# Attention of a two-block network: where the softmax is divided by its sums

## Chip, cores and metric

The kernel runs on one core of a Trainium2 chip, as one launch. The metric is device microseconds of that core. Three timed runs of the kernel before gave 3551.97, 3553.97 and 3556.66 us; the median, 3553.97 us, is the time before.

## The reference, cut to what matters

Two blocks of layers follow each other, each with mixers and feed-forward parts, on 512 tokens of width 1024 (and 256 context tokens in the second). The change touches only the attention of the second block, which comes in three kinds: a windowed one with a sink (layer 0), a neighbourhood one with a table of biases, and a global one (both layer 1). For each head all three compute the same thing:

```
s = q @ k.T * scale (+ bias or mask)       # 128 queries by n keys
e = exp(s - max(s));  sums = e.sum(-1) (+ exp(sink - max))
o = (e / sums) @ v                          # 128 queries by 64
```

A number divided before the product with `v` or after it gives the same `o`.

## The kernel before

Two heads times 128 queries are one unit of attention. There are 56 units: 24 windowed ones (line 1321; 256, 512 or 640 keys) and 32 of layer 1 (line 1715; 768 keys each, 16 with the table of biases and 16 global). A unit has three stages, and `step` (line 975) interleaves the stages of three units that follow each other: while one unit computes scores, the one before is transposed and the one before that is multiplied with the values.

- Scores (line 927), for each of the two heads: TensorE multiplies queries and keys into a PSUM tile `sc`; VectorE takes the maximum (lines 1006 to 1011); ScalarE writes the exponentials into `scratchP` and their sums beside it (line 1012), and in the windowed units the exponential of the sink (line 1014).
- Transposes (line 948): VectorE adds the sink's part (line 944), takes the reciprocal of one column of sums (line 945) and the numerators of each head are multiplied by it (line 946): by VectorE for the first head of a unit, by GpSimd for the second. Then TensorE transposes 128x128 blocks (line 325) into a PSUM tile `pt`, four to a piece, and ScalarE, or VectorE for the second piece of a unit (`ptv`), copies each piece into `scratchPT` (line 958).
- Values (line 960): TensorE multiplies the transposed blocks with the values into a PSUM tile `o` (line 322), in which the output stands transposed: 64 rows for each head by 128 queries. ScalarE copies it to SBUF (line 968; `bos` in the windowed units, `ox` in the others), and SyncE's queue stores it.

PSUM has two `sc` tiles in the windowed part and three in layer 1, two and one `pt`, and a single `o` (lines 1825 and 1867). `new_scratch` (line 984) cuts two large SBUF tiles into 5 slots for numerators and 8 for transposed pieces.

The windowed units run beside the first steps of a recurrence (`recurrence`, line 1345): its products `PM` on TensorE, its copies `M` and `W` on ScalarE and a long run of small VectorE operations on a tile `X` (lines 1440 to 1444). The units of layer 1 run alone, but for weights that are loaded ahead. The order of the instructions on each engine is not that of the source: the framework sorts them when it builds the program, and each engine then takes its own in that order.

Of the kernel before, what the change touches and what calls it, by code (L numbers as in the profile page):

```python
# [10 lines left out]
F32 = mybir.dt.float32  # L11
# [4 lines left out]
ALU = mybir.AluOpType  # L16
AX = mybir.AxisListType
PSUM = bass.MemoryType.PSUM
MUL, ADD, SUB = ALU.mult, ALU.add, ALU.subtract

D = 1024
KD = 8
S = 512
# [11 lines left out]
CTX = 256  # L35
T2 = S + CTX
# [84 lines left out]
class Kernel:  # L121
# [794 lines left out]
    def attention(self, active, qs, keys, vals, out, store, masks=(), **k):  # L916

        nc = self.nc  # L920
        P = [None, None]
        nb = len(vals[0])
        blocks = [(p, b) for p in range(2) for b in range(nb)]
        pieces = [blocks[i:i + 4] for i in range(0, 2 * nb, 4)]
        PT = {}

        def scores(p):
            sc = self.ps.tile([128, S + CTX], F32, tag="sc", name="sc", bufs=self.nsc)
            first = S
            for i, (kh, kl) in enumerate(keys[p][::-1]):  # L930
                if i:
                    first -= kh.shape[1]
                s = sc[:, S:] if i == 0 else sc[:, first:S]
                mk = masks if i else ()
                self.mm(s, qs[:, p, :], kh, start=True, stop=False)
                self.mm(s, qs[:, p, :], kl, start=False, stop=not mk)
                for j, (c, m) in enumerate(mk):
                    nc.tensor.matmul(s[:, c:c + 128], self.identb, m, start=False, stop=j == len(mk) - 1)
            P[p] = self.softmax(sc[:, first:], **{x: y[p] for x, y in k.items()})

        def normalised(p):
            P[p], a, es = P[p]
            if es is not None:
                nc.vector.tensor_tensor(a, a, es, ADD)
            nc.vector.reciprocal(a, a)
            (nc.gpsimd if p else nc.vector).tensor_scalar(P[p], P[p], a, None, op0=MUL)

        def transposed(i):
            pt = self.ps.tile([128, 512], F32, tag="pt", name="pt", bufs=self.npt)
            t = self.scratch("PT")  # L950
            for p, b in pieces[i]:
                if b == 0:
                    normalised(p)
            for j, (p, b) in enumerate(pieces[i]):
                self.tr(pt[:, 128 * j:128 * j + 128], P[p][:, 128 * b:128 * b + 128])
                PT[p, b] = t[:, 128 * j:128 * j + 128]
            w = slice(0, 128 * len(pieces[i]))
            (nc.vector.tensor_copy if i in self.ptv else nc.scalar.copy)(t[:, w], pt[:, w])

        def weighted(j):  # L960
            if j == 0:
                PT["o"] = self.ps.tile([128, 128], F32, tag="o", name="o", bufs=self.no)
            o = PT["o"]
            for b in range(2 * j, min(2 * j + 2, nb)):
                for p in range(2):
                    self.mm(o[64 * p:64 * p + 64, :], vals[p][b], PT[p, b], start=b == 0, stop=b == nb - 1)
            if 2 * j + 2 >= nb:
                nc.scalar.copy(out, o)
                if store:
                    nc.sync.dma_start(*store)  # L970

        active.append([[partial(f, i) for i in range(n)] for f, n in ((scores, 2), (transposed, len(pieces)), (weighted, (nb + 1) // 2))])
        self.step(active)

# [6 lines left out]
                if i < len(t):  # L981
                    t[i]()

    def new_scratch(self, **n):

        self.ring = {}
        for (name, k), tag in zip(n.items(), ("hThi", "hTlo")):
            W = self.hp.tile([128, KD * S], F32, tag=tag, name=f"scratch{name}")
            w = KD * S // k
            self.ring[name] = [W[:, w * j:w * j + w] for j in range(k)]  # L990

    def scratch(self, name):
        r = self.ring[name]
        r.append(r.pop(0))
        return r[-1]

    def softmax(self, sc, bias=None, nsink=None, sink=None, scale=None):

        nc, v = self.nc, self.nc.vector
        st = self.small.tile([128, 8], F32, tag="sm", name="sm", bufs=8)  # L1000
        mx, nm, sums, es = (st[:, i:i + 1] for i in range(4))
        n = sc.shape[1]
        P = self.scratch("P")[:, :n]

        if bias is not None:
            v.tensor_tensor_reduce(sc[:, :S], sc[:, :S], bias, 1.0, -3e38, op0=ADD, op1=ALU.max, accum_out=mx)
            v.reduce_max(es, sc[:, S:], axis=AX.X)
            v.tensor_scalar(nm, mx, es, -1.0, op0=ALU.max, op1=MUL)
        else:
            v.reduce_max(mx, sc, axis=AX.X, negate=True)  # L1010
            v.tensor_scalar(nm, mx, scale if nsink is None else nsink, None, op0=MUL if nsink is None else ALU.min)
        nc.scalar.activation(P, sc, AF.Exp, bias=nm, accum_out=sums, scale=1.0 if scale is None else scale)
        if sink is not None:
            nc.scalar.activation(es, sink, AF.Exp, bias=nm)
        return P, sums, es if sink is not None else None


    def store_split(self, x, dst, key=False):
# [768 lines left out]
    def block2(self, n, xd, out, stop=None, dbg=None):  # L1787
        nc, ap = self.nc, self.ap
# [19 lines left out]
        for i in range(2):  # L1808
            nt = NT2 if i == 0 else NT
            esM = ExitStack()  # L1810
            if i == 0:
                es = ExitStack()
                gemm_pools(es, "in0")
                self.ntmp = 1
                self.load_consts(3, self.act)
                self.load_consts(6, self.act)
                hT = self.hT2(n, mods)
                st = self.even(hT)
                es.close()
                es = ExitStack()  # L1820
                R = self.act = self.pool("R", es)
                self.load_consts(4, R)
                esW = ExitStack()
                other_psum(esW, "w")
                self.nsc, self.npt, self.no, self.npp, self.ptv = 2, 2, 1, 1, (1,)
                self.new_scratch(P=5, PT=8)
                windowed = self.windowed(st, R)
                next(windowed)
                rest = self.recurrence(st, R)
                for _ in range(4):  # L1830
                    next(windowed)
                next(rest)
                list(windowed)
                esW.close()
                self.npp = 2
                other_psum(es, "r")
                next(rest, None)
                self.hT = self.hT_tile()
                acc = self.new_acc()
                self.dn = ("w", 4)  # L1840
                self.mix_out(i, st, acc, 1, NT2)
                self.dn = ("dn", 2)
                next(rest, None)
                es.close()
                if stop in ("rw", "b"):
                    nc.sync.dma_start(dbg.rearrange("(i p) t -> i p t", p=128), st["out"][0 if stop == "rw" else 1])
                    esM.close()
                    es2.close()
                    return
                es = ExitStack()  # L1850
                gemm_pools(es, "o0")
                self.ntmp, self.nxt = 2, 4
            else:
                M = self.pool("M", esM)
                es = ExitStack()
                gemm_pools(es, "in1")
                self.ntmp, self.nhid = 2, 1
                self.load_consts(3, M)
                hT = self.hT2(n, mods)
                st = self.odd(hT, M)  # L1860
                mods = self.mods2(i, 3, V[f"g_pre_ff{i}"])
                es.close()
                es = ExitStack()
                R = self.pool("R1", es)
                other_psum(es, "a")
                self.act = R
                self.nsc, self.npt, self.no, self.ptv = 3, 1, 1, (1,)
                self.new_scratch(P=5, PT=8)
                self.odd_attention(st)
                es.close()  # L1870
                if stop in ("c", "d"):
                    nc.sync.dma_start(dbg.rearrange("(i p) t -> i p t", p=128), st["out"][0 if stop == "c" else 1])
                    esM.close()
                    es2.close()
                    return
                es = ExitStack()
                gemm_pools(es, "o1")
                self.ntmp, self.nxt = 2, 4
                self.hT = self.hT_tile()
# [11 lines left out]
            es = ExitStack()  # L1891
# [7 lines left out]
            n = self.ffn2(i, hT, nt, done)  # L1899
# [38 lines left out]
```

## Time and profile before

| | us |
|---|---|
| median of three timed runs | 3553.97 |
| the profiled execution | 3566.74 |
| its span, first to last instruction | 3565.0 |
| windowed units, by the trace | 1646 to 1790 |
| units of layer 1, by the trace | 2957 to 3139 |
| TensorE busy over the span | 3316.1 (93%) |
| VectorE, ScalarE, GpSimd busy | 2062.1, 1308.6, 504.1 |

All durations are those of the profiled execution, which took 1.74 us more than its span and 12.77 us more than the median. Matmuls are pipelined, so the duration of one says less than the distance from one to the next. TensorE is one queue of matmuls (PE) with a queue of weight loads (PEld) that runs ahead of it. [...]

### The profile page before, as it was taken

To read this page: it belongs to the slowest core of one execution; us is meant where nothing else is said; L and a number is where in the kernel's file an instruction comes from. 1 tells how busy PE (TensorE), PEld (TensorE's weight loads), DVE (VectorE), ACT (ScalarE), POOL (GpSimd) and SP (SyncE) were. 2 spreads that over 40 slices of the span, in tenths; PEclk is the share of its full clock that TensorE was granted. 3 is DMA by queue.
4 is the path that set the end of the run, shared out by engine and by line. 5 is a ranking of instruction groups with operands and counts; after the bars stand their busy time and mean duration, and the time that the engine had idled before them with its cause. 6 is when DMAs were issued, how large, how long until landed. Compare 5 with 4: busy or idle time off the path is not lost. (4 is left out here: it accounts for less than half of the span.)

```text
span 3565.0 us, 50330 instructions
## 1 busy us (share of the span) xinstructions
PE 3316.1 (93%) x19975; PEld 2638.1 (74%) x19975; DVE 2062.1 (58%) x3796; ACT 1308.6 (37%) x2150; POOL 504.1 (14%) x274
## 2 busy tenths in 40 slices
PE   8989999878999998988888899999999989999998
PEld 5677767746776777866587897888888777778887
DVE  4674554897745557686767667433334726653334
ACT  3243333327333334443542245422222525653222
POOL 0020000540200000123343331010000103410001
PEclk9999999989999998997988799999999999999999
DMA  7645565440456333445222124661221474143332
GB/s 249 193 143 167 171 219 176 133 142 12 123 175 208 108 105 109 113 117 170 52 73 68 50 71 165 144 154 54 68 63 62 135 208 153 37 131 106 95 95 83
DMA packets 520693, 436.66 MB, mean 122 GB/s; under 512 B 91924, under 2 KB 450042, under 8 KB 518922
## 3 DMA queue, kind: packets, MB, share of 16 engines
q1 hardware_dynamic: 520458, 433.45, 40.3%
q8 instruction: 157, 2.57, 0.3%
q14 instruction: 78, 0.64, 0.1%
HBM read 368.96 MB, written 63.78 MB: 121 GB/s over the span
## 5 line engine op out<-in xcount | busy, mean ns | idle before, releaser
L301 PE MATMUL dnps<-whi_dn,hidh 128*128 128x512 f32 x1120 | 449.0, 401 | 2.4 <-ACT hidh L276 1.2
L302 PE MATMUL dnps<-wlo_dn,hidh 128*128 128x512 f32 x1120 | 445.9, 398 | 0.0
L303 PE MATMUL dnps<-whi_dn,hidl 128*128 128x512 f32 x1120 | 443.4, 398 | 1.0 <-DVE hidl L277 1.0
L289 DVE TENSOR_TENSOR wlo_dn<-wraw_dn,whi_dn 128x1024 fp32r<-128x1024 f32 x136 | 167.3, 1231 | 249.8 <-ACT whi_dn L288 249.7
L301 PE MATMUL upps<-hThi,whi_up 128*128 128x512 f32 (+1 forms) x768 | 297.8, 390 | 5.3 <-DVE hThi L276 5.3
L302 PE MATMUL upps<-hTlo,whi_up 128*128 128x512 f32 (+1 forms) x768 | 295.2, 385 | 5.3 <-DVE hTlo L277 5.3
L303 PE MATMUL upps<-hThi,wlo_up 128*128 128x512 f32 (+1 forms) x768 | 294.2, 384 | 0.0
L423 DVE TENSOR_TENSOR acc<-dnps,acc 128x512 f32<-128x512 f32 x200 | 136.9, 688 | 213.4 <-PE dnps L303 212.9
L301 PEld LDWEIGHTS dnps<-whi_dn,hidh 128*128 128x128 f32 x1120 | 211.0, 188 | 64.6 <-ACT hidh L276 5.6
L288 ACT CAST whi_dn<-wraw_dn 128x1024 fp32r<-128x1024 f32 x140 | 147.1, 1051 | 283.9 <-PE dnps L303 105.5
L302 PEld LDWEIGHTS dnps<-wlo_dn,hidh 128*128 128x128 f32 x1120 | 211.3, 189 | 53.2 <-issue 2.7
L303 PEld LDWEIGHTS dnps<-whi_dn,hidl 128*128 128x128 f32 x1120 | 210.7, 189 | 53.2 <-DVE hidl L277 3.3
L302 PE MATMUL up2ps<-hTlo,whi_ff 128*128 128x512 f32 (+1 forms) x576 | 215.8, 375 | 5.0 <-DVE hTlo L277 4.7
L301 PE MATMUL up2ps<-hThi,whi_ff 128*128 128x512 f32 (+1 forms) x576 | 213.9, 373 | 2.3 <-DVE hThi L276 2.3
L303 PE MATMUL up2ps<-hThi,wlo_ff 128*128 128x512 f32 (+1 forms) x576 | 215.4, 375 | 0.0
L289 DVE TENSOR_TENSOR wlo_up<-wraw_up,whi_up 128x1024 fp32r<-128x1024 f32 x88 | 110.6, 1257 | 141.0 <-ACT whi_up L288 141.0
L301 PEld LDWEIGHTS upps<-hThi,whi_up 128*128 128x128 f32 x768 | 147.0, 192 | 54.5 <-issue 11.9
L302 PEld LDWEIGHTS upps<-hTlo,whi_up 128*128 128x128 f32 x768 | 147.5, 192 | 42.7 <-issue 9.9
L823 POOL TENSOR_TENSOR ag<-acc,gg 128x1024 f32<-128x1024 f32 x20 | 48.7, 2437 | 904.5 <-DVE acc L423 873.3
L303 PEld LDWEIGHTS upps<-hThi,wlo_up 128*128 128x128 f32 x768 | 147.8, 193 | 28.5 <-issue 0.8
L288 ACT CAST whi_ff<-wraw_ff 128x1024 fp32r<-128x1024 f32 x64 | 67.2, 1051 | 254.1 <-PE dnps L303 209.5
L289 DVE TENSOR_TENSOR wlo_ff<-wraw_ff,whi_ff 128x1024 fp32r<-128x1024 f32 x64 | 80.6, 1260 | 130.5 <-ACT whi_ff L288 130.1
(526 smaller groups left out, 7625.3 us busy)
## 6 DMA issues: line engine op xcount, KB each, us to landing
adaw<-in_w_ada_dram SPq DMA_DIRECT2D x96, 512.0 KB
wraw_up<-in_ffn_w_up_dram SPq DMA_DIRECT2D x88, 512.0 KB
wraw_ff<-in_w_ff_dram SPq DMA_DIRECT2D x64, 512.0 KB
wraw_dn<-in_w_ff_dram SPq DMA_DIRECT2D x64, 512.0 KB
adaw<-in_ffn_ada_w_dram SPq DMA_DIRECT2D x48, 512.0 KB
wraw_dn<-in_ffn_w_down_dram SPq DMA_DIRECT2D x44, 512.0 KB
adaw<-in_mix_ada_w_dram SPq DMA_DIRECT2D x32, 512.0 KB
ab<-ab SPq DMA_DIRECT2D x32, 384.0 KB
```

What stands on the lines that cost most here:

```text
L288: nc.scalar.copy(hi, raw)
L289: (eng or nc.vector).tensor_tensor(lo, raw, hi, SUB)
L301: mm(out, a[0], b[0], start=first, stop=False)
L302: mm(out, a[0], b[1], start=False, stop=False)
L303: mm(out, a[1], b[0], start=False, stop=last)
L423: nc.vector.tensor_tensor(acc[:, t, c], p, acc[:, t, c], ADD)
L823: nc.gpsimd.tensor_tensor(ag, a, gg[:, 0 if t < NT else 1, :], MUL)
```

## The change

The exponentials are no longer divided. They are transposed and multiplied with the values as they are. The sums of the two heads of a unit go side by side into a small tile `su`. At the start of the value stage VectorE adds the sink's part for both heads at once, and one reciprocal writes 128x128 elements into a new kind of slot, `R`: for each query the reciprocal of its sum, 64 times for each head. TensorE transposes that tile into the right half of the tile `o`, which grows from 128 to 256 columns, so that each row of the output finds its 128 divisors in its own row, and ScalarE copies it to a second `R` slot. After the value products VectorE multiplies `o` by it, in place of ScalarE's copy.

```
         def weighted(j):
             if j == 0:
-                PT["o"] = self.ps.tile([128, 128], F32, tag="o", name="o", bufs=self.no)
-            o = PT["o"]
+                PT["o"] = self.ps.tile([128, 256], F32, tag="o", name="o", bufs=self.no)
+
+                r = su[:, 0]
+                if "sink" in k:
+                    nc.vector.tensor_tensor(r, r, su[:, 1], ADD)
+                rt, PT["r"] = self.scratch("R"), self.scratch("R")
+                nc.vector.reciprocal(rt.rearrange("p (g c) -> p g c", g=2), r[:, :, None].to_broadcast([128, 2, 64]))
+                self.tr(PT["o"][:, 128:], rt)
+                nc.scalar.copy(PT["r"], PT["o"][:, 128:])
+            o = PT["o"][:, :128]
...
             if 2 * j + 2 >= nb:
-                nc.scalar.copy(out, o)
+                nc.vector.tensor_tensor(out, o, PT["r"], MUL)
```

```
-        def normalised(p):
-            P[p], a, es = P[p]
-            if es is not None:
-                nc.vector.tensor_tensor(a, a, es, ADD)
-            nc.vector.reciprocal(a, a)
-            (nc.gpsimd if p else nc.vector).tensor_scalar(P[p], P[p], a, None, op0=MUL)
...
-            for p, b in pieces[i]:
-                if b == 0:
-                    normalised(p)
```

`new_scratch` now takes the number of keys and cuts 5 slots for numerators of just that width; what is left of that tile becomes the `R` slots (2 in layer 1, 7 in the windowed part).

The framework sorts the instructions of both attention parts anew. Three places follow. The first is TensorE in the global half of layer 1, before (lines of the kernel before; `sc` are scores, `pt` transposes, `o` value products):

```order
L322 MATMUL o<-scratchPT,dv 64x128 x4
L322 MATMUL sc<-kh,qs 128x256
L322 MATMUL sc<-kl,qs 128x256
L325 MATMUL pt<-consts_73,scratchP 128x128 x4
L322 MATMUL o<-scratchPT,dv 64x128 x7
L322 MATMUL sc<-kh,qs 128x512
L325 MATMUL pt<-consts_73,scratchP 128x128 x4
L322 MATMUL o<-scratchPT,dv 64x128
```

The same engine and half after (numerators and `R` slots are both `scratchhThi` there, transposed pieces `scratchhTlo`):

```order
L325 MATMUL pt<-consts_73,scratchhThi 128x128 x4
L322 MATMUL o<-scratchhTlo,dv 64x128 x7
L322 MATMUL sc<-kh,qs 128x256
L322 MATMUL sc<-kl,qs 128x256
L325 MATMUL pt<-consts_73,scratchhThi 128x128 x4
L325 MATMUL o<-consts_73,scratchhThi 128x128
L322 MATMUL sc<-kh,qs 128x512
L322 MATMUL sc<-kl,qs 128x512
L322 MATMUL sc<-kh,qs 128x256
L322 MATMUL sc<-kl,qs 128x256
L322 MATMUL sc<-kh,qs 128x512
L325 MATMUL pt<-consts_73,scratchhThi 128x128 x4
```

The row `o<-consts_73,scratchhThi` is the new transpose of the reciprocals. Between the last value product of the unit before it and that row stand two score products of 256 columns and four transposes. The value products of a unit came in three runs before (4, 7 and 1 blocks); after, many come in two or in one.

The second place is VectorE in the same half, before (line 1010 is the maximum, 945 the reciprocal, 946 the multiplication of the numerators, 958 the copy of a piece):

```order
L1010 TENSOR_REDUCE sm<-sc 128x1
L945 RECIPROCAL sm<-sm 128x1
L1011 TENSOR_SCALAR sm<-sm,rq 128x1
L946 TENSOR_SCALAR scratchP<-scratchP,sm 128x768
L958 COPY scratchPT<-pt 128x512
```

And after, from the multiplication of one output to that of the next, and the reciprocal behind it:

```order
L967 TENSOR_TENSOR ox<-o,scratchhThi 128x128
L1008 TENSOR_SCALAR sm<-sm,rq 128x1 x2
L959 RECIPROCAL scratchhThi<-su 128x128
L949 COPY scratchhTlo<-pt 128x512
L1007 TENSOR_REDUCE sm<-sc 128x1
L1008 TENSOR_SCALAR sm<-sm,rq 128x1
L1007 TENSOR_REDUCE sm<-sc 128x1
L1008 TENSOR_SCALAR sm<-sm,rq 128x1
L967 TENSOR_TENSOR ox<-o,scratchhThi 128x128
L949 COPY scratchhTlo<-pt 128x512
L959 RECIPROCAL scratchhThi<-su 128x128
```

The reciprocal in the third of these rows belongs to the unit after the one whose output the ninth row multiplies: it stands most of a unit ahead of the transpose that reads it.

The third place is ScalarE in the windowed part, around two copies `W` of the recurrence that wait for a table of constants; before:

```order
L1012 ACTIVATE scratchP,sm<-sc,sm 128x512
L1014 ACTIVATE sm<-sink,sm 128x1
L1427 COPY W_14317<-consts_12860 64x8x64
L1427 COPY W_14318<-consts_12860 64x8x64
L958 COPY scratchPT<-pt 128x512
L1012 ACTIVATE scratchP,sm<-sc,sm 128x640
```

After:

```order
L1009 ACTIVATE scratchhThi,su<-sc,sm 128x512
L1011 ACTIVATE su<-sink,sm 128x1
L949 COPY scratchhTlo<-pt 128x512
L1424 COPY W_14293<-consts_12860 64x8x64
L1424 COPY W_14294<-consts_12860 64x8x64
L961 COPY scratchhThi<-o 128x128
L1379 COPY M_13025<-PM 128x4x64
L1009 ACTIVATE scratchhThi,su<-sc,sm 128x640
```

One copy of a transposed piece has moved from behind the two copies to ahead of them; the exponentials of the next unit are still behind.

## Rows read from the trace of the kernel before

**Rows 1.** The page: busy us, share of the span, instructions, by engine.
```profile
PE 3316.1 (93%) x19975; PEld 2638.1 (74%) x19975; DVE 2062.1 (58%) x3796; ACT 1308.6 (37%) x2150; POOL 504.1 (14%) x274
```
**Rows 2.** Windows: the windowed part in three stretches, layer 1 in two.
```profile
core 0: us, PE busy (x) PEld busy (x) DVE busy (x) ACT busy (x) POOL busy (x), PEclk, DMA share, GB/s
1646.00:1668.00 22.00, 10.00 (x59) 6.86 (x58) 12.66 (x38) 8.84 (x27) 5.92 (x11) 0.87 0.89 280
1668.00:1700.00 32.00, 31.71 (x232) 23.02 (x234) 13.80 (x40) 11.65 (x34) 9.65 (x7) 0.50 0.37 110
1700.00:1790.00 90.00, 70.55 (x582) 51.68 (x577) 61.95 (x228) 48.14 (x153) 29.91 (x24) 0.96 0.20 48
2957.00:3040.00 83.00, 78.77 (x614) 57.67 (x613) 61.53 (x192) 49.81 (x107) 33.42 (x15) 0.98 0.41 150
3040.00:3139.00 99.00, 95.31 (x800) 70.11 (x800) 61.51 (x133) 59.99 (x123) 38.69 (x17) 1.00 0.07 25
```
**Rows 3.** Instructions in time, 1662 to 1676: a stall in the windowed part.
```profile
1662.06 0.38 SPq L150 DMA_DIRECT2D consts<-in_consts_dram  x1
...
1666.37 1.26 ACT L1427 COPY W<-consts 64x512 f32<-64x512 f32 x2 [5.03 <-DMA consts<-in_consts_dram]
...
1668.29 0.69 PE L322 MATMUL o<-scratchPT,bvt 128*64 128x128 f32 x2 [5.66 <-ACT scratchPT L958]
```
**Rows 4.** Groups by line, whole span: busy, mean ns, idle before and releasers.
```profile
L325 PE MATMUL pt<-consts,scratchP 128*128 128x128 f32 x560 | 97.0, 292 | 19.6 <-POOL scratchP L946 16.8 <-DVE scratchP L946 1.1 <-DVE scratchPT L958 0.8
...
L945 DVE RECIPROCAL sm<-sm 128x1 f32<-128x1 f32 x112 | 17.5, 156 | 13.2 <-ACT scratchP L1012 12.8
...
L1215 DVE TENSOR_TENSOR bv<-bops,rows 128x256 f32<-128x256 f32 x4 | 1.7, 420 | 0.2 <-PE bops L1208 0.2
```
**Rows 5.** Waits of 1700 to 1790: us in total, times, longest.
```profile
PE pt L325 <- POOL scratchP L946: 15.1, 18, 1.8
```
**Rows 6.** The same view of 2957 to 3139.
```profile
PEld o L322 <- issue: 15.5, 87, 0.4
...
PE pt L325 <- POOL scratchP L946: 1.4, 3, 0.9
```
**Rows 7.** Groups by line of 2957 to 3139.
```profile
L946 POOL TENSOR_SCALAR scratchP<-scratchP,sm 128x768 f32<-128x768 f32 x32 | 72.1, 2254 | 195.5 <-DVE sm L945 181.6 <-DVE sm L1008 8.7 <-PE sc L322 3.0
...
L1010 DVE TENSOR_REDUCE sm<-sc 128x1 f32<-128x768 f32 x32 | 30.3, 955 | 14.1 <-PE sc L322 13.7
...
L946 DVE TENSOR_SCALAR scratchP<-scratchP,sm 128x768 f32<-128x768 f32 x32 | 22.3, 696 | 0.8
...
L958 DVE COPY scratchPT<-pt 128x512 f32<-128x512 f32 x32 | 22.0, 689 | 21.8 <-PE pt L325 21.7
...
L1007 DVE TENSOR_REDUCE sm<-sc 128x1 f32<-128x256 f32 x32 | 12.9, 416 | 0.1
...
L968 ACT COPY ox<-o 128x128 f32<-128x128 f32 x32 | 8.6, 267 | 10.3 <-PE o L322 10.0
```
**Rows 8.** Chain of waits of 2957 to 3040: start us, us, what.
```profile
2976.11 0.59 PE pt L325 x4
```
**Rows 9.** Instructions in time, 1674.9 to 1676, TensorE at the low clock.
```profile
1675.00 1.11 PE L325 MATMUL pt<-consts,scratchP 128*128 128x128 f32 x4
```
**Rows 10.** Chain of waits of 3036 to 3139.
```profile
3037.21 1.02 PE o L322 x14
```
**Rows 11.** VectorE's groups, 1640 to 1800, one row.
```profile
L1196 DVE TENSOR_TENSOR ab<-kd,einv 128x384 f32<-128x384 f32 x2 | 5.8, 2922 | 0.0
```
**Rows 12.** Instructions in time, 3134.9 to 3137: waits for the one tile `o`.
```profile
3135.80 0.43 PE L322 MATMUL o<-scratchPT,dv 128*64 128x128 f32 x2 [0.35 <-ACT ox L968]
```
**Rows 13.** Instructions in time, 3120 to 3140: score products at the full clock.
```profile
3121.84 0.28 PE L322 MATMUL sc<-kh,qs 128*128 128x256 f32 x1
...
3121.96 0.28 PE L322 MATMUL sc<-kl,qs 128*128 128x256 f32 x1
```

More of the change, by code (lines that the diff above doesn't have):

```diff
@@ L925, in attention @@
         PT = {}
+        su = self.small.tile([128, 2, 2], F32, tag="su", name="su", bufs=5)
         def scores(p):
@@ L938, in scores @@
                     nc.tensor.matmul(s[:, c:c + 128], self.identb, m, start=False, stop=j == len(mk) - 1)
-            P[p] = self.softmax(sc[:, first:], **{x: y[p] for x, y in k.items()})
-        def normalised(p):
-            P[p], a, es = P[p]
-            if es is not None:
-                nc.vector.tensor_tensor(a, a, es, ADD)
-            nc.vector.reciprocal(a, a)
-            (nc.gpsimd if p else nc.vector).tensor_scalar(P[p], P[p], a, None, op0=MUL)
+            P[p] = self.softmax(sc[:, first:], su[:, 0, p:p + 1], su[:, 1, p:p + 1], **{x: y[p] for x, y in k.items()})
         def transposed(i):
@@ L982, in step, with new_scratch @@
                     t[i]()
[L984 to L990, printed above, removed]
+    def new_scratch(self, n):
+        P, PT = (self.hp.tile([128, KD * S], F32, tag=tag, name=f"scratch{tag}") for tag in ("hThi", "hTlo"))
+        cut = lambda W, a, b, w: [W[:, j:j + w] for j in range(a, b, w)]
+        self.ring = dict(P=cut(P, 0, 5 * n, n), R=cut(P, 5 * n, KD * S, 128), PT=cut(PT, 0, KD * S, 512))
     def scratch(self, name):
@@ L995, in scratch, with softmax @@
         return r[-1]
-    def softmax(self, sc, bias=None, nsink=None, sink=None, scale=None):
+    def softmax(self, sc, sums, es, bias=None, nsink=None, sink=None, scale=None):
         nc, v = self.nc, self.nc.vector
         st = self.small.tile([128, 8], F32, tag="sm", name="sm", bufs=8)
-        mx, nm, sums, es = (st[:, i:i + 1] for i in range(4))
+        mx, nm, mc = (st[:, i:i + 1] for i in range(3))
         n = sc.shape[1]
@@ L1006, in softmax @@
             v.tensor_tensor_reduce(sc[:, :S], sc[:, :S], bias, 1.0, -3e38, op0=ADD, op1=ALU.max, accum_out=mx)
-            v.reduce_max(es, sc[:, S:], axis=AX.X)
-            v.tensor_scalar(nm, mx, es, -1.0, op0=ALU.max, op1=MUL)
+            v.reduce_max(mc, sc[:, S:], axis=AX.X)
+            v.tensor_scalar(nm, mx, mc, -1.0, op0=ALU.max, op1=MUL)
         else:
@@ L1014, in softmax @@
             nc.scalar.activation(es, sink, AF.Exp, bias=nm)
-        return P, sums, es if sink is not None else None
+        return P
     def store_split(self, x, dst, key=False):
@@ L1825, in block2 @@
                 self.nsc, self.npt, self.no, self.npp, self.ptv = 2, 2, 1, 1, (1,)
-                self.new_scratch(P=5, PT=8)
+                self.new_scratch(3 * 128 + CTX)
                 windowed = self.windowed(st, R)
@@ L1867, in block2 @@
                 self.nsc, self.npt, self.no, self.ptv = 3, 1, 1, (1,)
-                self.new_scratch(P=5, PT=8)
+                self.new_scratch(T2)
                 self.odd_attention(st)
```

## The prediction

> **What bounds the kernel now.** I read the page first: TensorE is busy for 93% of the span, GpSimd for 14% [rows 1]. The change touches two stretches, so next come the windows, which show three regimes [rows 2]. [...] In the windowed part from 1700 to 1790 it is busy for 70.6 of 90 us, and so are none of the others (VectorE 62.0, ScalarE 48.1, GpSimd 29.9): engines wait for each other. [...]
>
> The waits say for whom TensorE idles. Over the whole span the transposes stood 19.6 us behind somebody: 16.8 us behind GpSimd's multiplication of the numerators and 1.1 us behind VectorE's [rows 4]; 15.1 us of it, in 18 waits of 1.8 us at most, lie between 1700 and 1790 [rows 5], and only 1.4 us in layer 1 [rows 6], though GpSimd does 32 such operations of 2254 ns there [rows 7].
>
> **TensorE's new work.** One transpose is added to each unit. Four follow each other in 0.59 us at the full clock [rows 8], 0.148 us each, and in 1.11 us at the low one [rows 9], 0.278 us each. Of 56 I put 6 into the low stretch (56 units, 24 of them in 144 us, so 5 to 6 in 32 us): 50 x 0.148 + 6 x 0.278 = +9.1 us. Nothing hides it in layer 1; in the windowed part it may fall into gaps, so its ends are +5 and +9, and I take +9.1.
>
> **Waits that go.** No transpose waits for a multiplication any more: -16.8 - 1.1 = -17.9 us. What is late next is the exponentials, one GpSimd or VectorE operation earlier, then the copies of the pieces and the next scores, which come no earlier than before. In the windowed stretch, where nobody is full, I let a third of the 15.1 us come back as other waits: +5.0 us; the ends are 0 and +15.1.
>
> **Runs of value products.** Value products follow each other every 0.073 us (14 in 1.02 us) [rows 10], but when a run of them begins the weight load idles for about 15.5/87 = 0.18 us with nobody named [rows 6]. Counting runs in the two orders over both parts gives 142 before and 113 after, so 29 fewer: -29 x 0.18 = -5.2 us. A weight load that idles need not hold up the matmuls, so the ends are 0 and -5.2; I take the full value, since in layer 1 there is no other gap for it to hide in.
>
> **VectorE.** Removed from a unit of layer 1: two reciprocals of one column, 156 ns each [rows 4], and one multiplication, 696 ns [rows 7]. Added: a product of 128 columns from PSUM and SBUF and a reciprocal of 128 columns. For the product, the row for 256 columns has 420 ns [rows 4]; by element the maxima give (955 - 416) / 512 = 1.05 ns [rows 7], so 420 - 128 x 1.05 = 286 ns. No reciprocal of more than one column is in the trace. From below it is 156 ns; at one element per step of 1.05 ns it is 156 + 127 x 1.05 = 289 ns; from above I take the slowest VectorE row by element near this part, 2922 / 384 = 7.6 ns [rows 11], which gives 156 + 127 x 7.6 = 1.12 us. The row of the same operation says nothing on width, so I take the ordinary step, 0.29 us. Then VectorE loses 312 + 696 and gains 286 + 289 ns: 0.43 us less in a unit, and by the same kinds of operations about as much in a windowed one. It has gaps everywhere [rows 2], so I book nothing for this; at 1.12 us it would have 0.40 us more in a unit.
>
> **ScalarE, GpSimd, queues.** ScalarE loses a copy of 128x128 (267 ns) [rows 7] and gains one of the same shape: zero. It now waits for the new transpose where it waited for the last value product. GpSimd loses all 56 operations; nobody needs it more. SyncE's queue has the output stores of the windowed part at other places between loads that run three units ahead: zero, as long as a store is not late.
>
> **The new wait.** There is one tile `o`, so the transpose of the reciprocals has to wait until the output of the unit before is multiplied. Before, ScalarE's copy held it the same way: at the end of layer 1 TensorE waited 0.35 us for a copy of 0.27 us [rows 12], 0.08 us more than the copy. Now it is 0.29 us plus two such hand-overs, about 0.45 us. In the order shown, TensorE has two score products of 256 columns and four transposes in between: 2 x 0.12 [rows 13] + 0.59 = 0.8 us. The reciprocal itself stands most of a unit ahead. So the wait is covered: zero, with the condition that nothing slow stands before the multiplication on VectorE.
>
> **The stall.** It ends when the constants arrive, whatever is ahead of it. One piece more is copied before it, but the next exponentials stay behind: zero. The low stretch after it I leave as it is: zero.
>
> **Sum.** 9.1 - 17.9 + 5.0 - 5.2 = -9.0 us. On the profiled execution 3566.74 becomes 3557.7; its 12.8 us above the median have nothing to do with the change, so the median goes from 3554.0 to 3545.
>
> **Rivals.**
>
> The wide reciprocal is slow. At 1.12 us VectorE has 0.40 us more in each unit instead of 0.43 less. For it: no row excludes it. Against its cost: VectorE idles 28 of 90 us in the windowed stretch, 21 of 83 and 37 of 99 in layer 1 [rows 2], and the reciprocal stands far ahead. In the first two stretches the 18 + 16 units get 34 x 0.83 = 28 us more than in my sum; if a third of that shows, +9 us: 3554, no change.
>
> [...]
>
> The single tile `o` becomes a ring. Multiplication on VectorE, transpose, ScalarE's copy and value products of one unit must be over before the next begins, and the multiplication queues in order behind a maximum (955 ns) and a copy (689 ns) that the sorting may put before it [rows 7]. If both have just begun, the transpose is late by 0.96 + 0.69 + 0.45 - 0.8 = 1.3 us; if this happens in every third unit, 19 x 1.3 = +25 us: 3570. Against it: the order shown has neither directly ahead with work still to come, and the old ring cost almost nothing. It decides where TensorE has no more than those 0.8 us of work between the last value product and the new transpose.
>
> [...]
>
> **Chances.** My forecast 0.42, slow reciprocal 0.28, ring 0.17, shorter low stretch 0.13. What the measurement can tell from no change is 0.2%, 7.1 us. Faster: three quarters of the forecast, a quarter of the slow reciprocal and all of the last: 0.51. Slower: a tenth of the slow reciprocal and nearly all of the ring: 0.19. The rest, 0.30, is the same. Range: from the last rival with some waits less, 3528, to the ring, 3570.
>
> **What would show it.** In the profile after: the `pt` row has no wait for GpSimd, and its idle time is 5 to 8 us instead of 19.6; a row of `o` from the constants, 56 times; VectorE's reciprocal near 0.29 us, or near 1.1 us for the first rival; the wait of the new transpose for VectorE near zero, or over 15 us for the ring; the windowed part some 10 us shorter and layer 1 between 2 us shorter and 3 us longer. I am wrong if layer 1 grows by more than 6 us, or if the windowed part's waits are all there again under other names.

## The result, and the profile after

| | us |
|---|---|
| before, median of 4 runs | 3555.31 (3551.97 to 3556.88) |
| after, median of 4 runs | 3501.64 (3494.01 to 3508.97) |
| ratio, 95% interval | 0.9849 (0.9831 to 0.9867) |
| profiled execution: span before, after | 3565.0, 3507.2 |

The kernel is 53.7 us faster; 9 were forecast, and 3501.6 lies below the range of 3528 to 3570. The page after, against [rows 1]: TensorE has 56 instructions more and is busy for 66 us less.

```profile
PE 3250.3 (93%) x20031; PEld 2627.8 (75%) x20031; DVE 2074.5 (59%) x3716; ACT 1306.9 (37%) x2150; POOL 397.9 (11%) x218
```

So large a fall can't come from two stretches with 286 us of matmuls, and it doesn't. The first score product of the windowed part comes at 1634.2 us, where it came at 1647.2: 13.0 us are gained before the change has executed anything. Behind layer 1 the rest of the program takes 418.1 us for 426.0, again the same code. The instructions in time show how. In a row of products of 512 columns TensorE starts 30 of them in 2428.49 - 2421.46 = 7.03 us before, 234 ns each:

```profile
2421.46 0.40 PE L301 MATMUL dnps<-whi_dn,hidh 128*128 128x512 f32 x1
...
2428.49 0.40 PE L301 MATMUL dnps<-whi_dn,hidh 128*128 128x512 f32 x1
```

And after, the same products at the same clock (1.00), 6.80 us, 227 ns each:

```profile
2385.39 0.39 PE L301 MATMUL dnps<-whi_dn,hidh 128*128 128x512 f32 x1
...
2392.19 0.39 PE L301 MATMUL dnps<-whi_dn,hidh 128*128 128x512 f32 x1
```

Now the two stretches that were changed. The windows after, in the places of [rows 2] (columns as there): ahead of the low clock, the low clock, the rest of the windowed part, and the two halves of layer 1.

```profile
1634.00:1657.00 23.00, 13.91 (x87) 10.96 (x87) 13.40 (x31) 9.41 (x28) 2.45 (x7) 0.70 0.90 305
1657.00:1678.00 21.00, 21.00 (x166) 16.26 (x165) 9.48 (x17) 9.11 (x25) 3.81 (x3) 0.51 0.37 97
1678.00:1767.00 89.00, 70.52 (x649) 54.34 (x650) 70.88 (x209) 50.83 (x160) 2.72 (x7) 0.98 0.23 54
2911.00:2993.00 82.00, 77.66 (x630) 58.60 (x628) 65.42 (x175) 49.72 (x108) 0.00 (x0) 0.98 0.42 150
2993.00:3089.00 96.00, 91.42 (x811) 69.48 (x809) 63.46 (x117) 56.64 (x119) 0.00 (x0) 1.00 0.08 26
```

PEclk is the clock that TensorE was granted, as a share of its full speed. The long stretch at the low clock has 21 us (0.51) instead of 32 (0.50); the stretch behind it has TensorE idle for 18.5 of 89 us, as before (19.4 of 90). The groups by line answer to [rows 4]: the transposes `pt` stand longer than before, 26.0 us for 19.6, now behind ScalarE's exponentials; the new transposes of `o` hardly stand; the wide reciprocal takes 947 ns.

```profile
L325 PE MATMUL pt<-consts,scratchhThi 128*128 128x128 f32 x560 | 100.2, 296 | 26.0 <-ACT scratchhThi L1009 21.9 <-ACT scratchhTlo L949 1.9 <-DVE scratchhTlo L949 1.9
L325 PE MATMUL o<-consts,scratchhThi 128*128 128x128 f32 x56 | 16.4, 293 | 2.7 <-DVE bos L967 2.2 <-DVE scratchhThi L959 0.4
L959 DVE RECIPROCAL scratchhThi<-su 128x128 f32<-128x128 f32 x56 | 53.0, 947 | 4.8 <-PE o L325 3.7 <-ACT scratchhTlo L949 0.7
```

The waits of the windowed part (1634 to 1767; us in total, times, longest), against [rows 5], show the link behind: the exponentials in turn wait for the scaled maximum on VectorE's queue.

```profile
ACT scratchhThi L1009 <- DVE sm L1008: 22.2, 18, 3.8
PE pt L325 <- ACT scratchhThi L1009: 19.9, 19, 3.7
```

The stall of [rows 3] has shrunk: 1.48 us on ScalarE for 5.03, and TensorE idles 1.81 us for another transfer instead of 5.66. Just ahead of it, though, TensorE has idled 3.74 us for exponentials.

```profile
1648.73 0.38 SPq L150 DMA_DIRECT2D consts<-in_consts_dram  x1
...
1649.46 1.12 PE L325 MATMUL pt<-consts,scratchhThi 128*128 128x128 f32 x4 [3.74 <-ACT scratchhThi L1009]
...
1652.68 1.26 ACT L1424 COPY W<-consts 64x512 f32<-64x512 f32 x2 [1.48 <-DMA consts<-in_consts_dram]
...
1655.84 0.68 PE L322 MATMUL PM<-AB 64*64 64x64 f32 x16 [1.81 <-DMA AB<-ab]
```

In layer 1 (2911 to 3089) the weight load's idle time with nobody named, [rows 6], falls from 15.5 us in 87 pieces to 10.5 in 62:

```profile
PEld o L322 <- issue: 10.5, 62, 0.2
```

### The profile page after: what moved, and what is told of

It reads as the page before. It is cut to its first block, busy times and chain, and to the rows that moved or that the text cites. A ratio compares the mean times of both kernels' runs of the same rounds, so it can differ in the third digit from the quotient of the medians.

```text
span 3507.2 us, 50216 instructions
## 1 busy us (share of the span) xinstructions
PE 3250.3 (93%) x20031; PEld 2627.8 (75%) x20031; DVE 2074.5 (59%) x3716; ACT 1306.9 (37%) x2150; POOL 397.9 (11%) x218
## 5 line engine op out<-in xcount | busy, mean ns | idle before, releaser
L303 PE MATMUL dnps<-whi_dn,hidl 128*128 128x512 f32 x1120 | 435.6, 391 | 1.1 <-DVE hidl L277 1.1
L301 PEld LDWEIGHTS upps<-hThi,whi_up 128*128 128x128 f32 x768 | 147.3, 193 | 51.8 <-issue 11.9
L289 DVE TENSOR_TENSOR wlo_ff<-wraw_ff,whi_ff 128x1024 fp32r<-128x1024 f32 x64 | 80.9, 1265 | 126.0 <-ACT whi_ff L288 125.7
```

The costliest lines, as they stand in the source:

```text
L289: (eng or nc.vector).tensor_tensor(lo, raw, hi, SUB)
L301: mm(out, a[0], b[0], start=first, stop=False)
L303: mm(out, a[1], b[0], start=False, stop=last)
```

## The experiments

**Where the tiles lie.** The five tiles `su` take 160 bytes in the small pool, and the build puts every SBUF tile behind that pool, the activations among them, 160 bytes higher; the weights lie ahead of it and stay. Of a product's two operands one is loaded into TensorE (the queue PEld; 128x128 in 188 to 193 ns each in before), the other, 512 columns wide, is streamed over it: a down product streams weights over loaded activations, an up product the other way round. The first kernels add nothing but unused tiles:

```
+        self.small.tile([128, 4], F32, tag="pad", name="pad", bufs=5)   # 32 bytes each: b_pad160; 1 to 4 of them: b_pad32 to b_pad128; 3 in the changed kernel: a_pad96
```

> The kernel before with five small tiles of 32 bytes that nothing uses, where the change has its five tiles su: every SBUF tile behind them lies 160 bytes higher, as in the changed kernel, and no instruction differs. Theory A (placement): the step from one 512-column matmul to the next falls from 234 ns (down products) and 232 ns (up products) to 227 ns in the whole program, as it did with the change, and the time from 3555 to about 3517 us (3510 to 3524): 58 us less in the profiled span, of which some 11 us fell into the windowed part, 3.5 us into layer 1's attention and some 5 us into the recurrence. Rival B (the attention's own change, by its order, its clock or its DMAs, makes everything else faster): 234 and 232 ns and 3555 us.

> The changed kernel with 96 bytes more of small tiles that nothing uses, so that everything behind them lies 256 bytes higher than in the kernel before instead of 160. Theory A, if the place counts modulo 256 bytes or a smaller power of two: steps of 234 and 232 ns as before, and 3502 + 38 = 3540 us (3533 to 3547); what is left of the gain, some 15 us, is the attention's. Theory A with another period, and rival B: 227 ns and 3502 us.

> The kernel before with one unused tile of 32 bytes, everything behind it 32 bytes higher. If the place counts modulo 64 (160 and 32 are the same modulo 64 and modulo 128): steps of 227 ns, and about 3517 us. If it counts modulo 256: 160 is not the same as 32, and the steps are 234 ns or something in between. Rival B: 234 ns, 3555 us.

> The kernel before with two unused tiles, everything behind them 64 bytes higher. If the place counts modulo 64: steps of 234 and 232 ns and 3555 us. If it counts modulo 128 or 256: another step than that of the kernel before, between 227 and 234 ns. Rival B: 234 ns, 3555 us.

> The kernel before with three unused tiles, everything behind them 96 bytes higher. So far the step depends on where the streamed operand lies against the loaded one, modulo 256 bytes: 227 ns at 0, 232 at 128, 234 at 160, and 231, 232, 237 in turn at 96. Here the down products are at 64 and the up products at 192. Theory A (the relation decides): a step of its own for each, between 227 and 237 ns, and between 3527 and 3560 us. Rival C (only a few absolute places of the activations are good): the same step in both.

> The kernel before with four unused tiles, 128 bytes higher: the down products at 32, the up products at 224. Theory A: steps between 227 and 237 ns; if distance from 0 counts, these two are the nearest to it and the steps nearest to 227. Rival C: the same step in both kinds.

In the seventh kernel the unused bytes lie ahead of weights and activations alike:

```
         self.load_consts(0, self.const)
+        self.const.tile([128, 24], F32, name="pad")
```

> The kernel before with 96 unused bytes ahead of the weight tiles, so that weights and activations both lie 96 bytes higher: weights at 0 and activations at 96 modulo 256. Theory A (the relation decides, and that is as before): 234 ns in the down products, 231, 232, 237 in turn in the up products, and 3556 us (3550 to 3562). Rival C (the absolute place of one of the two decides): other steps than before.

Measured. Place is the streamed operand's address less the loaded one's, modulo 256 bytes; the step is the median distance between the starts of products of 512 columns that follow each other (three values: it alternates). Times without an interval are of one run, with the median of before, taken beside them, in brackets.

| kernel | place, down / up | step down, ns | step up, ns | us |
|---|---|---|---|---|
| before | 160 / 96 | 234 | 231, 232, 237 | |
| b_pad32 | 128 / 128 | 232 | 232 | 3547.0 (3556.9) |
| b_pad64 | 96 / 160 | 231, 232, 237 | 234 | 3560.5 (3556.9) |
| b_pad96 | 64 / 192 | 229 | 233 | 3532.2 (3556.8) |
| b_pad128 | 32 / 224 | 234 | 233 | 3553.9 (3556.8) |
| b_pad160 | 0 / 0 | 227 | 227 | 3527.5; 0.9916 (0.9901 to 0.9931) |
| b_const96 | 160 / 96 | 234 | 231, 232, 237 | 3563.3 (3556.8) |
| after | 0 / 0 | 227 | 227 | 3501.6; 0.9849 (0.9831 to 0.9867) |
| a_pad96 | 160 / 96 | 234 | 231, 232, 237 | 3536.7; 0.9947 (0.9930 to 0.9963) |

Theory A holds. b_pad160 executes what the kernel before executes and is 29.4 us faster (38 were expected, and 3527.5 lies above the range); a_pad96 executes what the changed kernel executes and is 35.0 us slower, with exactly the steps of before, so the place counts modulo 256. An estimate from the steps alone is larger: some 4000 long products of each kind at 7 and 5 ns less would be 48 us. The granted clock of b_pad160's four runs is 0.950 to 0.954 against 0.954 to 0.957 before, which would take back a part; the rest is not explained. The relation decides, not an absolute place: b_const96 moves both operands and changes nothing, b_pad64 swaps the patterns of down and up products because it swaps their places, and b_pad96 has two different steps in one program, 6.88 us for 30 down products (229 ns) and 6.99 for 30 up products (233 ns):

```profile
3108.12 0.40 PE L301 MATMUL dnps<-whi_dn,hThi 128*128 128x512 f32 x1
...
3115.00 0.39 PE L301 MATMUL dnps<-whi_dn,hThi 128*128 128x512 f32 x1
...
3252.05 0.39 PE L301 MATMUL up2ps<-hThi,whi_ff 128*128 128x512 f32 x1
...
3259.04 0.39 PE L301 MATMUL up2ps<-hThi,whi_ff 128*128 128x512 f32 x1
```

That a place near 0 is a good one did not hold: 32 is as slow as 160. Products of 256 columns do not follow this order: the up products `up2ps` of that width have a median step of 114 ns in b_pad96 and 117 to 120 in the others, 120 at 0 / 0. That may be why b_pad96 has nearly the time of b_pad160 with longer steps; no run tests it. Layer 1's attention has 181.4 to 181.6 us in before and the six kernels that move tiles: the operands of its scores and value products move together or not at all, and its transposes, where only one moves, have 128 columns.

**The attention at one place.** Everything below lies at 0 / 0, so b_pad160 with 3527.5 us is its "before", and the changed kernel gains 25.9 us on it (20.2 at the other place, a_pad96 against before). First the kernel before without any division:

```
-            nc.vector.reciprocal(a, a)
-            (nc.gpsimd if p else nc.vector).tensor_scalar(P[p], P[p], a, None, op0=MUL)
```

> The kernel before at the place of the changed kernel (160 bytes higher), with the reciprocals and the multiplications of the numerators left out: no division by the sums at all, and nothing in its place. Against the 3527 us of that place: by the terms of the prediction the waits that go give 17.9 us and 5.0 come back, so 3514 us (3509 to 3519); the changed kernel, with its 56 transposes, products and wide reciprocals, would then be slower than this, but it had 3502. Rival D (the new transposes cost what was said, and the waits that go are worth far more): 3492 us. Rival E (the waits that go are worth 25 us and the new work costs nothing): 3502 us.

3490.4 us, 0.9802 (0.9778 to 0.9826): rival D. Taking the division out is worth 37 us, and putting it back behind the value products costs 11. Next, the price of the wide reciprocal:

```
-                nc.vector.reciprocal(rt..., r[:, :, None].to_broadcast([128, 2, 64]))
+                nc.vector.reciprocal(r, r)
+                nc.vector.tensor_copy(rt..., r[:, :, None].to_broadcast([128, 2, 64]))    # a_recip2p: nc.gpsimd
```

> The changed kernel with a reciprocal of the two columns of sums and a copy on VectorE that spreads them to 128 columns, in place of the reciprocal of 128 columns (947 ns). By 156 ns for a narrow reciprocal and some 0.25 us for the copy, VectorE has 56 x 0.54 = 30 us less, 13 us of it in the windowed part. Theory F (the wide reciprocal is what the windowed part pays for: without a division it is 115.8 us long, with the new work 132.5): windowed part some 125 us, 3494 us (3488 to 3498). Rival G (VectorE has gaps and the reciprocal stands ahead: it costs nothing): 3502 us (3498 to 3506).

> As a_recip2, but GpSimd makes the copy that spreads the two reciprocals, so VectorE has only 0.16 us of it. Theory F: 3491 us (3485 to 3497), a little below a_recip2 if VectorE's time decides; rival G: 3502; above 3506 if GpSimd's copy arrives late for the new transpose, which then waits for GpSimd as the old ones did.

3506.7 us, 0.9859 (0.9834 to 0.9883), and 3507.7, 0.9864 (0.9843 to 0.9885): no gain, so theory F failed. Both lie just above rival G's 3498 to 3506; above 3506 was the sign of a late copy in a_recip2p, and there the new transposes wait 1.4 us for GpSimd. The trace of a_recip2 shows that the reciprocal was not free: the exponentials' wait for VectorE falls from 22.2 to 14.6 us and TensorE's for them from 19.9 to 16.0 (1629.7 to 1754.0), with 161 + 223 ns in place of 947. That gain is too small to stand out of the runs' spread of 11 to 15 us.

```profile
ACT scratchhThi L1010 <- DVE sm L1009: 14.6, 13, 3.8
PE pt L325 <- ACT scratchhThi L1010: 16.0, 16, 3.7
```

Most of the time that VectorE saves it spends in another wait: ahead of adding the sink's part it stands 14.2 us for ScalarE in a_recip2, and stood 6.0 in the changed kernel.

```profile
DVE su L957 <- ACT su L1012: 14.2, 11, 4.2
```

In the changed kernel:

```profile
DVE su L957 <- ACT su L1011: 6.0, 7, 1.8
DVE bos L967 <- PE o L322: 8.1, 9, 2.4
```

Then the stall:

```
-                nc.scalar.copy(AD[q]..., c["eye"][half(q), None, :].to_broadcast([64, 8, 64]))
+                nc.scalar.copy(AD[q]..., c["ident"][half(q), None, half(q)].to_broadcast([64, 8, 64]))
```

> The kernel before, 160 bytes higher (3527 us), where ScalarE's two copies W read the unit matrix from the constants of the start and not from the table that arrives late: the wait of 5.03 us on ScalarE's queue is gone, all else computes the same. Theory H (the stall keeps TensorE's clock low for the 30 to 37 us behind it): the low clock in the windowed part falls from 42 to 51 us to under 30, its length from 143 to some 128, 3513 us (3507 to 3518). Rival I (the stall costs its 5 us and the clock stays as it is): 3522 us (3519 to 3527).

> The changed kernel with the same edit; there ScalarE waited only 1.5 us for the table and TensorE 1.8 us for another transfer. Theory H: most of what b160_eye gains has already come with the change, so 3500 us (3495 to 3503). Rival I: 3501 us. If both lose as much as each other (5 us or more), the stall was worth the same in both and explains nothing of the change.

3517.8 us, 0.9896 (0.9873 to 0.9920), and 3503.4, 0.9851 (0.9822 to 0.9880). In the kernel before the edit gained 9.7 us where theory H had 14. The time alone does not decide between H (up to 3518) and rival I (from 3519), as the four runs reach from 3515.5 to 3525.0; the clock in the table below speaks for H, with a mean of 0.90 in the windowed part instead of 0.82 (one execution each). In the changed kernel the edit alone gained nothing. Last, GpSimd itself:

```
-            (nc.gpsimd if p else nc.vector).tensor_scalar(P[p], P[p], a, None, op0=MUL)
+            nc.vector.tensor_scalar(P[p], P[p], a, None, op0=MUL)
```

> The kernel before, 160 bytes higher (3527 us), with all numerators multiplied on VectorE and none on GpSimd. Theory J (what cost was GpSimd's multiplication of 1.5 us in the windowed part and 2.25 in layer 1, against VectorE's 0.5 and 0.7): TensorE's wait for GpSimd, 15.8 us, goes and a wait for VectorE of 3 to 5 us takes its place; the windowed part at the full clock's pace from 118 to some 108 us, 3515 us (3508 to 3520). Rival K (VectorE, with 12 us more in the windowed part and 22 more in layer 1, is late with all else): the same idle time of TensorE under VectorE's name, 3527 us or more.

> b160_dve with the unit matrix from the constants of the start as in b160_eye (which alone gave 10 us). If the two gains are of different things they add: 3527 - 12 - 10 = 3505 us (3499 to 3511), as fast as the changed kernel without a single new transpose. If both are the same low stretch of the clock: 3513 us (3510 to 3518).

> The changed kernel (3502 us) with the narrow reciprocal, GpSimd's copy and the unit matrix from the constants of the start. Each alone gave 3503 to 3508. If the changed kernel waits for the exponentials, as its rows say (19.9 us), none of the three is on its path: 3502 us (3497 to 3508). If they hid each other: below 3495.

3504.3 us, 0.9856 (0.9829 to 0.9883): theory J, with twice its gain and below its range. TensorE waits 4.3 us for the multiplication where it had waited 15.8. That GpSimd slowed VectorE's other work is not the reason: the maxima over 640 columns take 821 ns in b_pad160 and 820 here.

```profile
PE pt L325 <- DVE scratchP L947: 4.3, 8, 0.7
```

b160_dve_eye has 3491.5 us, 0.9816 (0.9789 to 0.9843): the two gains add up (23.2 and 9.7 us alone, 35.9 together), so the edit of the stall gives 12.8 us here. a_recip2p_eye has 3492.5, 0.9829 (0.9799 to 0.9859), below 3495 as expected if the three edits hid each other. Against a_recip2p the edit of the stall gives 15.2 us there. Both kernels have lower medians than the changed kernel, but the intervals overlap with its own.

What the windowed part (first score product to last output) and layer 1 took, each in its profiled execution; length x clock is what the stretch would have at a clock of 1.00 throughout if all of it followed the clock. Idle time need not follow it, so this is a rough measure:

| kernel | windowed | PEclk | length x clock | layer 1 |
|---|---|---|---|---|
| before | 143.0 | 0.84 | 120.1 | 181.5 |
| b_pad160 | 143.4 | 0.82 | 117.6 | 181.5 |
| b160_eye | 134.7 | 0.90 | 121.2 | 181.5 |
| b160_undiv | 115.9 | 0.88 | 102.0 | 177.8 |
| b160_dve | 125.9 | 0.86 | 108.3 | 179.6 |
| b160_dve_eye | 119.9 | 0.90 | 107.9 | 178.7 |
| after | 132.4 | 0.86 | 113.9 | 178.4 |
| a_pad96 | 121.2 | 0.94 | 113.9 | 177.2 |
| a_eye | 126.0 | 0.89 | 112.1 | 177.2 |
| a_recip2 | 124.3 | 0.90 | 111.9 | 180.0 |
| a_recip2p_eye | 118.1 | 0.94 | 111.0 | 176.2 |

The rows of four of them, by windows; b_pad160:

```profile
1628.80:1772.20 143.40, 114.81 (x867) 84.11 (x868) 86.81 (x304) 68.59 (x212) 45.28 (x40) 0.82 0.34 96
```

b160_undiv:

```profile
1628.00:1743.90 115.90, 98.65 (x868) 75.02 (x868) 68.50 (x184) 68.30 (x212) 10.47 (x16) 0.88 0.42 119
```

b160_dve:

```profile
1629.10:1755.00 125.90, 107.93 (x868) 78.38 (x868) 92.92 (x328) 69.31 (x212) 10.78 (x16) 0.86 0.39 109
```

after:

```profile
1634.20:1766.60 132.40, 104.98 (x892) 81.23 (x892) 93.53 (x256) 68.96 (x212) 8.64 (x16) 0.86 0.37 104
```

TensorE is idle for 28.6, 17.3, 18.0 and 27.4 us of them. The changed kernel's gain here is not in idle time. The clock swings from one execution to the next (132.4 us at 0.86 and 121.2 at 0.94 for the same instructions in after and a_pad96, both 113.9 by the product), so a length by itself says little.

## Why the prediction was wrong, point by point

**The sum lacked its largest term.** The step that failed is "The change touches two stretches": the sum was made over their instructions and waits and took everything else as unchanged. The place of the tiles gave 29.4 us by b_pad160 and 35.0 by a_pad96, more than half of the 53.7. The diff held the cause, five tiles in the small pool, and the prediction spoke of `su` only as an operand. The order of instructions can't show it. At the place of before the changed kernel has 3536.7 us (a_pad96), inside the range, 20.2 us below before where 9 were forecast.

**Waits that go: the price was right, what the new work on VectorE brings back was not booked.** No transpose waits for a multiplication any more, as said. In the windowed part I had 15.1 us behind GpSimd and about 1 behind VectorE; b160_undiv is 117.6 - 102.0 = 15.6 us shorter by the product. Its idle time falls by 28.6 - 17.3 = 11.3 us, so for the division alone the third that I let come back was about right. In the changed kernel nearly all came back (27.4 us idle), 19.9 us of it behind the exponentials (10.2 in b160_undiv): the sign of being wrong that I had named, the waits all there again under other names, came true. The term that failed is VectorE's, for which I booked nothing because "it has gaps everywhere". I had named the exponentials as next in line and said that they come no earlier; they come later than in b160_undiv, as ScalarE waits 22.2 us for VectorE's maxima and 10.4 there:

```profile
ACT scratchP L1009 <- DVE sm L1008: 10.4, 15, 1.6
PE pt L325 <- ACT scratchP L1009: 10.2, 11, 2.3
```

VectorE is busy for 93.5 of 132.4 us after and 68.5 of 115.9 without the division. The new work costs the windowed part 113.9 - 102.0 = 11.9 us, of which 24 transposes at 0.148 are 3.6. The reciprocal accounts for 2 more (111.9 in a_recip2). In the changed kernel VectorE stands 8.1 us for the value products ahead of its multiplication of the output (row above), a wait that it did not have before; whether that or another move delays the maxima is not settled.

**GpSimd was the larger part of the trouble.** The prediction's own row had it: 16.8 of the 17.9 us of waits stood behind GpSimd. b160_dve keeps the division where it was, changes one engine and reaches 3504.3 us: a gain of 23.2 us, without a new transpose, where the change has 25.9. Leaving the division out gains 37.1, so 13.9 stay with the division on VectorE.

**The stall.** "It ends when the constants arrive, whatever is ahead of it ... zero" failed. It ended with the constants, but in the changed kernel ScalarE comes to it later and waits 1.48 us, and TensorE has transposes and scores to do in the meantime. Not all of that is the order's: in b_pad160, with the old order, ScalarE waits only 3.2 us in place of before's 5.03. b160_eye puts the stall at 10 us. a_eye finds none of it left, but a_recip2p_eye gains 15.2 us on a_recip2p by the same edit, so what it is worth in the changed kernel is open.

```profile
ACT W L1428 <- DMA consts<-in_consts_dram: 3.2, 1, 3.2
```

**The low stretch** got shorter, to which I had given a chance of 0.13. My 12 us at most for it, from which the lower end of the range came, is an estimate that no run shows: it takes the work to go with the clock, so that the 32 us at 0.50 [rows 2] are 16 us of work at 1.00, or 20 us at the pace of the stretch behind (70.6 busy of 90). Four transposes took 1.11 us at the low clock and 0.59 at the full one [rows 8, rows 9]. Of the windowed part's 143.4 - 132.4 = 11.0 us, 3.7 are the product's and 7.3 the clock's; in a_pad96 against before 6.2 and 15.6. It is more than the swing: by the clock records the seven executions of the old instructions (before, the five b_pad, b_const96) have 42.2 to 51.2 us at a granted clock of 0.50 in the windowed part, after and a_pad96 37.5 and 13.7. The stall looks like one cause (0.90 in b160_eye), but not the only one: b160_undiv still has it in full (5.77 us on ScalarE, 5.41 on TensorE) and runs at a mean of 0.88, against 0.82. What else it was is open.

```profile
1647.19 1.26 ACT L1424 COPY W<-consts 64x512 f32<-64x512 f32 x2 [5.77 <-DMA consts<-in_consts_dram]
...
1649.59 0.69 PE L322 MATMUL PM<-AB 64*64 64x64 f32 x8 [5.41 <-DMA AB<-ab]
```

**TensorE's new work and the runs of value products** held for layer 1 in the main, where TensorE was busy for 78.8 of 83 and 95.3 of 99 us before, at a clock of 0.98 and 1.00 [rows 2]. 32 transposes at 0.148 us are +4.7 (a dear row: most pieces of four in that chain have 0.44 us, 0.11 each); the value products' busy time there falls by 6.2 us, from 35.3 + 34.8 before:

```profile
L322 PE MATMUL o<-scratchPT,dv 128*64 128x128 f32 x384 | 35.3, 283 | 0.9 <-ACT ox L968 0.7
L322 PE MATMUL o<-scratchPT,cv 128*64 128x128 f32 x384 | 34.8, 283 | 0.0
```

to 31.9 + 32.0 after:

```profile
L322 PE MATMUL o<-scratchhTlo,cv 128*64 128x128 f32 x384 | 32.0, 283 | 0.0
L322 PE MATMUL o<-scratchhTlo,dv 128*64 128x128 f32 x384 | 31.9, 282 | 0.7 <-ACT scratchhThi L961 0.7
```

Layer 1 is 3.1 us shorter (4.3 in a_pad96), a little more than the -2 that I allowed. Over both parts the new work costs 3501.6 - 3490.4 = 11.2 us, and that this is near +9.1 is luck: by the table 11.9 fall into the windowed part, mostly not transposes, and 178.4 - 177.8 = 0.6 into layer 1.

**The wide reciprocal** has 947 ns, not 0.29 us: the ordinary step was the wrong choice, and the end from above, 1.12 us, nearly right. The slow-reciprocal rival had the size and not the effect (3554): the times with the narrow form alone show no gain. With the stall gone it may have one: a_recip2p_eye is 10.9 us below a_eye, but the intervals overlap.

**The ring through the one tile `o`** did not come: 2.7 us in 56 waits.

Added up at one place, from profiled executions of b_pad160 and after: windowed -11.0, layer 1 -3.1, and the recurrence behind the windowed part 369.3 to 361.7, -7.6 at a clock of 0.88 and 0.90. The last I can't tie to the change: a_eye has 367.0 there. The stretch ahead of the windowed part, the same code, is 5.4 us longer after, and the profiled spans differ by 3524.6 - 3507.2 = 17.4. The timed difference is 25.9.

## What to carry to other kernels

Before explaining a result, line up the stretches that the change does not touch: if they moved, look at where the tiles lie, and give both kernels the same addresses before comparing anything else. A new small tile can be worth more than the edit that needed it (here the place gave 29.4 us, the edit 25.9). Where an engine waits for a slow one, first give the same work to the fast one: it is one word, and here it gained 23.2 us where the new algorithm gained 25.9.

## What the runs showed of the hardware

- The step of TensorE's 512-column products depends on the places of its two operands against each other, modulo 256 bytes (a_pad96 has the steps of before): 227 ns at 0 (b_pad160, after), 229 at 64 (b_pad96), 232 at 128 (b_pad32), and 233 to 234 on average at 32 and 224 (b_pad128), 96 and 160 (before, b_pad64, b_const96, a_pad96) and 192 (b_pad96). The products of 256 columns do not follow it (114 ns at 192, b_pad96; 120 at 0). Why the step changes is open.
- A reciprocal of 128 columns takes 947 ns, 7.4 ns an element; of 2 columns 161 ns, and VectorE's copy that spreads them 223 ns (the first in after, the others in a_recip2).
- GpSimd's copy of the same 128x128 elements takes 308 ns (24 of them in the windowed part of a_recip2p) against VectorE's 223, where its multiplication of 768 columns took 2254 ns against VectorE's 696 [rows 7].
